# Ranking slots of stored tiles later in the free list of a hybrid decoder kernel

## The chip, the cores and the metric

The kernel runs on one core of a Trainium2 chip. The metric is the device time of one execution in microseconds (us); the time before is 1214.88 us, the median of three runs.

## The reference

One decoder layer is applied to x (1024 positions by 1024 channels, fp32). A normalised and modulated input goes through one wide projection. Its columns feed two gated linear recurrences in parallel (HGRN2 with 8 heads, GLA with 4 heads). Each branch is normalised, gated and projected, the branches are merged by sigmoid gates, projected once more, added to x and normalised.

```python
h = rms_norm(x, norm_w[l]) * (1.0 + scale[:, None, :]) + shift[:, None, :]
proj = h @ w_in[l]
hq, hf, hi, hz, gq, gk, gv, gz, ga, mg = jnp.split(proj, IN_OFFSETS, axis=-1)
y_h = hgrn2_branch(hq, hf, hi, hz, lb_all[l], hgrn_norm_w[l])
y_g = gla_branch(gq, gk, gv, gz, ga, gla_alpha_w[l], gla_alpha_b[l], gla_norm_w[l])
u_h = y_h @ w_branch[l, 0]
u_g = y_g @ w_branch[l, 1]
mg = jax.nn.sigmoid(mg.reshape(B, T, N_BRANCH, D_MODEL))
merged = mg[:, :, 0] * u_h + mg[:, :, 1] * u_g
x = x + gate[:, None, :] * (merged @ w_out[l])
return rms_norm(x, final_norm_w)
```

Inside a branch the recurrence S_t = diag(a_t) S_{t-1} + k_t v_t^T, o_t = S_t^T q_t is computed in chunks.

## The kernel before

**Arithmetic.** Every large product is made from three matmuls on operands that are split into a rounded high part and a remainder. `split` (L191) does it for one tile: a ScalarE cast (L196) makes the high part, a VectorE subtraction (L197) the low part. In the last stages the same is done by `build` (cast L1263, subtraction L1264) and `prep_duo` (cast L1285, subtraction L1286), for blocks that are multiplied in seven products instead of eight; for these, sums and differences of blocks are made earlier and kept in memory.

**Storage.** Nearly all working tiles of SBUF come from 46 slots of 128 partitions by 4 KB. `Slots.get` takes the slot at the head of a list of free slots, `Slots.free` puts slots back at its end, so the slot that was free longest is taken first. `Halves` hands out halves of such a slot. All this happens while the program is written, not while it runs. The tile framework then makes the first instruction that writes a new tile wait for the last instruction that used the slot before, also for the landing of a store that still reads it.

**Order.** After an opening that is written by hand, the framework orders the instruction lists of TensorE (PE), VectorE (DVE), ScalarE (ACT), GpSimd (POOL) and SyncE (SP, which issues the loads) by times that it plans for them. Which slot a tile has enters this plan, since it decides on whom the tile's first writer waits.

**Stages.** `Stream` (L857) runs one projection job after another, PE's matmuls being L541 (feature tiles) and L600 to L602 and L643 to L645 (value tiles). It weaves two other tracks between them: the attention of the heads (`attention`, L657; PE scores L683, L715, L770, L776, L781; DVE work on them L690 to L759), and a background track with `factors` (L1155: loads of stored activations, differences L1166, stores L1167) and `weight_sums` (L1183: loads L1189, sums L1195 to L1199, stores L1201). The last stages (from about 750 us) multiply the blocks (L1343), take snapshots of PSUM banks (`snap_of`, L1315 and L1317), and apply the gates (L1414).

**Stores.** Five places write a tile to memory and give its slot back at once, while the store is still to run: `put_act` (L914, results yh and yg of a branch), `factors`, `weight_sums`, `put_gate1` (L1412, a gate) and `drop_wy` (L1487, sums of the output weights). All are issued by POOL.

Of the kernel before, what the change touches and what calls it, by code (L numbers as in the profile page):

```python
# [2 lines left out]

# [31 lines left out]
class Slots:  # L35


    def __init__(self, pool, n):
        self.pool = pool
        self.free_list = deque(range(n))  # L40
        self.owner = {}
        self.serial = 0

    def get(self, shape, dtype=F32):
        i = self.free_list.popleft()
        self.serial += 1
        t = self.pool.tile([P] + list(shape), dtype, tag=f"s{i}", name=f"b{self.serial}")
        self.owner[id(t)] = (i, t)
        return t

    def free(self, *tiles):
        for t in tiles:
            self.free_list.append(self.owner.pop(id(t))[0])


class Halves:
# [5 lines left out]
    def get(self):  # L62
        if not self.open:
            t = self.slots.get([2, 512])
            left = [0, t]
            self.open.extend((t[:, i, :], left) for i in range(2))
        v, left = self.open.popleft()
        left[0] += 1
        self.owner[id(v)] = (v, left)
        return v  # L70

    def free(self, *views):
        for v in views:
            v, left = self.owner.pop(id(v))
            left[0] -= 1
            if left[0]:
                self.open.append((v, left))
            else:
                self.open = deque(z for z in self.open if z[1] is not left)
                self.slots.free(left[1])  # L80


@with_exitstack
def hybrid_trunk_kernel(
# [7 lines left out]
    x2, o2 = x[0], out[0]  # L92
# [8 lines left out]
    S = Slots(sp, N_SLOTS)  # L101
    Q = Halves(S)
# [811 lines left out]
    def put_act(acts, d, y):  # L914
        for half in range(2):
            nc.gpsimd.dma_start(acts[half][d // 2][:, d % 2 * 512:d % 2 * 512 + 512], y[:, half * 512:half * 512 + 512])
        S.free(y)

    def alpha_side():
        lower_bound()  # L920
# [49 lines left out]
    def gla_attention(h):  # L970
        qk = g_state
        v = qk.pop(("v", h))
        g = {}
        sq = {}

        def post(vh, half, po):
            if half == 0:
                g[vh] = qk.pop(("z", h, vh))
                sq[vh] = S.get([T])
            sl = slice(half * 512, half * 512 + 512)  # L980
            nc.scalar.activation(sq[vh][:, sl], po, AF.Square)
            nc.vector.scalar_tensor_tensor(g[vh][:, sl], po, vec[:, R_GN + vh:R_GN + vh + 1],
                                           g[vh][:, sl], ALU.mult, ALU.mult)

        yield from attention(qk.pop(("q", h)), qk.pop(("k", h)), alphas[h], lambda: v, 0, 256, post)
        S.free(*v)
        nc.gpsimd.tensor_add(sq[0], sq[0], sq[1])
        yield 1.5
        rst = sq[1]
        yield from inverse_root(rst, sq[0], 256)  # L990
        for half in range(4):
            sl = slice(half * 256, half * 256 + 256)
            for vh in range(2):
                nc.vector.tensor_mul(g[vh][:, sl], g[vh][:, sl], rst[:, sl])
            yield 1.5
        for vh in range(2):
            put_act(yg_d, 2 * h + vh, g[vh])
        S.free(*sq.values())
# [142 lines left out]
    def part_of(acts, kh, half, kk):  # L1141
        return acts[half][kh * 2 + kk]
# [12 lines left out]
    def factors(acts, f):  # L1155
        sub = nc.vector.tensor_sub
        for kk in range(2):
            while len(S.free_list) < 12:
                yield 1
            y = {}  # L1160
            for b in ("12", "11", "22", "21"):
                y[b] = S.get([T])
                nc.sync.dma_start(y[b], part_of(acts, int(b[0]) - 1, int(b[1]) - 1, kk))
            yield 6
            for p, dst, a, b in ((5, "11", "12", "11"), (7, "12", "12", "22"), (6, "22", "22", "11"), (4, "21", "21", "22")):
                sub(y[dst], y[a], y[b])  # L1166
                nc.gpsimd.dma_start(f[p][kk], y[dst])  # L1167
                if p == 7:
                    S.free(y["12"])
                elif p == 6:  # L1170
                    S.free(y["11"])
                yield 1.5
            S.free(y["22"], y["21"])

    def branch(n, d):
        return w_branch[0, n, :, d * P:(d + 2) * P]
# [6 lines left out]
    def weight_sums(b, i):  # L1183
        src = sources[b][i]
        while len(S.free_list) < 12:
            yield 1
        x1, x2 = S.get([4, 2, P]), S.get([4, 2, P])
        for kh, x in enumerate((x1, x2)):
            nc.sync.dma_start(x.rearrange("p k a f -> p k (a f)"),  # L1189
                              src[kh * 512:(kh + 1) * 512, :].rearrange("(k p) f -> p k f", p=P))  # L1190
        yield 6
        s1, s2 = S.get([2, 4, P]), S.get([2, 4, P])
        parts = {5: s1[:, 0], 6: s1[:, 1], 3: s2[:, 0], 7: s2[:, 1]}
        add = nc.vector.tensor_add
        add(parts[7], x1[:, :, 0], x1[:, :, 1])  # L1195
        add(parts[5], x1[:, :, 1], x2[:, :, 1])
        yield 1.5
        add(parts[6], parts[7], x2[:, :, 1])
        add(parts[3], parts[6], x2[:, :, 0])  # L1199
        for p, q in SUMS.items():  # L1200
            nc.gpsimd.dma_start(w_sums[b][i // 2][q][:, i % 2 * 512:i % 2 * 512 + 512],  # L1201
                                parts[p].rearrange("p k f -> p (k f)"))
        S.free(x1, x2, s1, s2)
        yield 3

    def prepare():
        yield from factors(h_d, f_x)
        for b in range(4):
            for i in range(4):
                yield from weight_sums(b, i)  # L1210
# [79 lines left out]
    class Banks:  # L1290
# [11 lines left out]
        def free(self, v):  # L1302
            self.free_list.append(v)
# [108 lines left out]
    def put_gate1(d, half, ap, summed):  # L1412
        g = ap if summed else Q.get()
        nc.scalar.activation(g, ap, AF.Sigmoid)  # L1414
        nc.gpsimd.dma_start(gate1_d[d][:, half * 512:half * 512 + 512], g)
        Q.free(g)

    def put_gate0(d, half, ap, summed):
        nc.scalar.activation(merged(d, half), ap, AF.Sigmoid)
# [13 lines left out]
    def put_m(d, half, ap, summed):  # L1433
# [16 lines left out]
    for g in BUILT[1:]:  # L1450
        n = GROUPS.index(g)
# [8 lines left out]
    wy, w4_raw, W4 = {}, {}, {}  # L1460
# [24 lines left out]
        keep_wy(p, kk, *dst)  # L1485

    def drop_wy():  # L1487
        S.free(*wy.values())
        wy.clear()

    def load_w4(p):
# [97 lines left out]
    for kk, (lead, first, then) in enumerate((((0, 3, 0), (0, 6), (0, 7)), ((1, 1, 2), (1, 5), (1, 6)))):  # L1589
        after(*lead, lambda kk=kk: load_wy(kk))  # L1590
        after(*((1, 1, 0) if kk == 0 else (1, 7, 3)), drop_wy)
        for n in range(4):
            after(*first, n, lambda kk=kk, n=n: gate_wy(kk, n))
            after(*then, n, lambda kk=kk, n=n: sum_wy(kk, n))
# [124 lines left out]
```

## Time and profile before

| what | value |
|---|---|
| three runs | 1214.5, 1214.88, 1215.29 us |
| profiled execution, own time | 1216.46 us |
| its span | 1214.8 us |
| granted TensorE clock, mean | 0.998 |
| PE busy | 1184.1 us, 97% of the span |
| DVE busy | 790.9 us, 65% |
| ACT busy | 546.9 us, 45% |
| POOL busy | 123.8 us, 10% |
| moved by DMA | 183.51 MB, 151 GB/s on average |

The profiled execution's own time exceeds its span by 1.66 us and the median of the three runs by 1.58 us. Times of instructions are those of this one execution. A row of the timeline gives start, duration, engine, source line and operation, then the tiles written and read without their numbers, and in brackets how long the engine sat idle before it and for whom. Adjacent instructions of one engine overlap by about 0.1 us.

### The profile page before, as it was taken

What the parts mean: (1) busy time and instruction counts of PE and PEld (TensorE: products, weight loads), DVE (VectorE), ACT (ScalarE), POOL (GpSimd) and SP (SyncE); (2) the same over time, 40 slices, a digit from 0 to 9 for tenths busy, and PEclk for the clock granted to TensorE, in tenths of its full rate; (3) what the DMA queues carried; (4) which work ended last, traced back from release to release, by engine and by line L of the source; (5) the groups of instructions that cost most, each with busy time, mean ns of one, the idle gap of its engine ahead of it and who ended that gap; (6) DMA issues with size and microseconds to landing.
All of it is one profiled execution on the core that took longest, in us unless ns stands there. A gap on an engine that the chain in (4) does not pass through costs nothing.

```text
span 1214.8 us, 20860 instructions
## 1 busy us (share of the span) xinstructions
PE 1184.1 (97%) x8579; PEld 982.6 (81%) x8579; DVE 790.9 (65%) x1245; ACT 546.9 (45%) x797; POOL 123.8 (10%) x215
## 2 busy tenths in 40 slices
PE   5999999999999999999999999999999999999997
PEld 3777889889798888888887888877778888878886
DVE  4637444774848456877884365794653775988994
ACT  5646732434434244344332324455743544444554
POOL 4100000202111121121110101011220000000000
PEclk9999999999999999999999999999999999999999
DMA  9814000844444267255341112054697746435523
GB/s 320 277 70 139 18 19 19 293 141 161 156 152 149 66 207 249 94 179 169 108 174 47 59 53 70 36 174 158 227 343 277 260 160 208 135 104 173 174 104 122
DMA packets 130961, 183.51 MB, mean 151 GB/s; under 512 B 7467, under 2 KB 97633, under 8 KB 130866
## 3 DMA queue, kind: packets, MB, share of 16 engines
q1 hardware_dynamic: 117250, 136.87, 35.7%
q0 software_dynamic: 13568, 45.31, 9.6%
q8 instruction: 67, 1.10, 0.4%
q14 instruction: 28, 0.23, 0.1%
q10 hardware_dynamic: 48, 0.01, 0.0%
HBM read 132.87 MB, written 49.28 MB: 150 GB/s over the span
## 4 chain that ended last, share of the span: by engine, by line
PE 61%; issue 23%; DVE 3%; ACT 3%; POOL 2%; DMA 1%; POOLq 0%; ACTq 0%; DVEq 0%
PE pd L541 19%; PE pd L1343 9%; PE sc_ps L1343 5%; PE pm L1343 5%; PE pd L1520 3%; PE pd L643 2%; PE pd L644 2%; PE pd L645 2%; PE sc_ps L1520 2%; PE pm L848 1%; PE pd L352 1%; PE pm L829 1%; PE pm L850 1%; PE pm L1520 1%; PE sc_ps L352 1%
## 5 line engine op out<-in xcount | busy, mean ns | idle before, releaser
L541 PE MATMUL pd<-b,b 128*128 128x512 f32 x1632 | 387.4, 394 | 0.0
L541 PEld LDWEIGHTS pd<-b,b 128*128 128x128 f32 x1632 | 302.4, 188 | 64.8 <-issue 1.4
L1343 PE MATMUL pd<-b,b 128*128 128x512 f32 x720 | 173.7, 392 | 4.3 <-ACT b L1414 2.1
L1343 PEld LDWEIGHTS pd<-b,b 128*128 128x128 f32 x720 | 133.7, 188 | 35.7 <-ACT b L1414 3.2
L197 DVE TENSOR_TENSOR b<-b,b 128x1024 fp32r<-128x1024 f32 (+2 forms) x89 | 98.9, 1122 | 83.1 <-ACT b L196 65.4
L196 ACT CAST b<-b 128x1024 fp32r<-128x1024 f32 (+2 forms) x89 | 82.9, 948 | 92.1 <-DVE b L1199 14.6
L1286 DVE TENSOR_TENSOR b<-b,b 128x1024 fp32r<-128x1024 f32 x56 | 68.3, 1224 | 66.9 <-ACT b L1285 52.3
L1285 ACT CAST b<-b 128x1024 fp32r<-128x1024 f32 x56 | 58.3, 1050 | 73.9 <-PE pd L1343 20.6
L1343 PE MATMUL sc_ps<-b,b 128*128 128x512 f32 x324 | 79.4, 391 | 1.0 <-ACT scT L793 1.0
L600 PE MATMUL pd<-b,b 128*128 128x256 f32 x256 | 74.2, 290 | 0.0
L1264 DVE TENSOR_TENSOR b<-b,b 128x1024 fp32r<-128x1024 f32 x48 | 59.2, 1251 | 20.8 <-ACT b L1263 15.1
L602 PE MATMUL pd<-b,b 128*128 128x256 f32 x256 | 72.5, 283 | 0.0
L601 PE MATMUL pd<-b,b 128*128 128x256 f32 x256 | 72.4, 283 | 0.0
L1343 PEld LDWEIGHTS sc_ps<-b,b 128*128 128x128 f32 x324 | 60.3, 188 | 14.6 <-ACT scT L793 1.4
L1343 PE MATMUL pm<-b,b 128*128 128x512 f32 x300 | 72.1, 389 | 0.0
L1263 ACT CAST b<-b 128x1024 fp32r<-128x1024 f32 x48 | 49.9, 1050 | 41.2 <-PE pd L1343 16.0
L1343 PEld LDWEIGHTS pm<-b,b 128*128 128x128 f32 x300 | 56.3, 188 | 11.7
L352 PE MATMUL pd<-b,b 128*128 128x512 f32 x192 | 53.3, 410 | 2.0 <-ACT b L196 0.9
L1201 POOL DMA_DIRECT2D ws<-b x64 | 34.6, 541 | 192.0 <-DVE b L1195 86.5
L735 ACT COPY xb<-b 128x512 f32<-128x512 f32 x48 | 29.4, 620 | 49.4 <-PE sc_ps L715 26.7
L643 PE MATMUL pd<-b,b 128*128 128x512 f32 x128 | 51.3, 401 | 0.0
L644 PE MATMUL pd<-b,b 128*128 128x512 f32 x128 | 50.0, 390 | 0.0
(285 smaller groups left out, 1964.3 us busy)
## 6 DMA issues: line engine op xcount, KB each, us to landing
b<-in_w_in_dram SPq DMA_DIRECT2D x66, 512.0 KB, 4.2
ws<-b POOLq DMA_DIRECT2D x64, 256.0 KB, 3.3
b<-ws SPq DMA_DIRECT2D x32, 512.0 KB, 4.9
b<-in_x_dram SPq DMA_DIRECT2D x16, 512.0 KB, 5.7
b<-in_ada_w_dram SPq DMA_DIRECT2D x32, 256.0 KB, 6.9
b<-in_w_branch_dram SPq DMA_DIRECT2D x16, 512.0 KB, 4.4
b<-h SPq DMA_DIRECT2D x14, 512.0 KB, 4.3
wo<-b POOLq DMA_DIRECT2D x14, 512.0 KB, 5.7
```

The lines of the kernel that those rows point to most:

```text
L196: nc.scalar.copy(hi, src)
L197: nc.vector.tensor_sub(lo, src, hi.bitcast(F32))
L352: nc.tensor.matmul(accs[f], wg(a, d, f), b[d][:, half * 512:half * 512 + 512], start=(d == 0 and n == 0), stop=(d == KT - 1 and n == 2))
L541: nc.tensor.matmul(ps[0:w, th * 512:(th + 1) * 512], a[:, k, 0:w], b[:, th * 512:(th + 1) * 512], start=(k == 0 and n == 0), stop=(k == KT ...
L600: nc.tensor.matmul(o, lh, hi[:, k % 4, :], start=(k == 0), stop=False)
L601: nc.tensor.matmul(o, lh, lo[:, k % 4, :], start=False, stop=False)
L602: nc.tensor.matmul(o, ll, hi[:, k % 4, :], start=False, stop=(k == KT - 1))
L643: nc.tensor.matmul(o, lh, hi[:, k % 2, :], start=(k == 0), stop=False)
L644: nc.tensor.matmul(o, lh, lo[:, k % 2, :], start=False, stop=False)
L1286: nc.vector.tensor_sub(lo, t, hi.bitcast(F32))
L1343: nc.tensor.matmul(o, a[:, sl], c, start=(p in (1, 5) and kt == 0 and n == 0), stop=(kt == 3 and n == 2), skip_group_check=True)
L1520: nc.tensor.matmul(o, a, b, start=(p in (1, 5) and kt == 0 and n == 0), stop=(kt == 3 and n == 2), skip_group_check=True)
```

## The change

The list of free slots becomes a heap. A slot's rank is the count of tiles taken so far when it is given back; slots of tiles that were given back behind a store to memory (`sent=True`) have 8 added to it, so they rank behind slots that are given back up to eight takings later. Among equal ranks, the one given back first goes first. The number of slots, the moments at which tiles are taken and given back, and thus every count of free slots, are as before.

```diff
     def get(self, shape, dtype=F32):
-        i = self.free_list.popleft()
+        i = heapq.heappop(self.free_list)[-1]
...
-    def free(self, *tiles):
+    def free(self, *tiles, sent=False):
         for t in tiles:
-            self.free_list.append(self.owner.pop(id(t))[0])
+            self.freed += 1
+            heapq.heappush(self.free_list, (self.serial + (8 if sent else 0), self.freed, self.owner.pop(id(t))[0]))
...
     def put_act(acts, d, y):
...
-        S.free(y)
+        S.free(y, sent=True)
...
                 if p == 7:
-                    S.free(y["12"])
+                    S.free(y["12"], sent=True)
                 elif p == 6:
-                    S.free(y["11"])
+                    S.free(y["11"], sent=True)
                 yield 1.5
-            S.free(y["22"], y["21"])
+            S.free(y["22"], y["21"], sent=True)
...
-        S.free(x1, x2, s1, s2)
+        S.free(x1, x2)
+        S.free(s1, s2, sent=True)
...
-        Q.free(g)
+        Q.free(g, sent=True)
...
     def drop_wy():
-        S.free(*wy.values())
+        S.free(*wy.values(), sent=True)
```

`Halves.free` passes the mark on: a slot counts as sent if one of its two halves was. Of 853 tiles taken, 78 are given back as sent, and 272 tiles get a slot with another history than before. The first of them is b_2258, a load that SP issues at 238.00 us in the profile before.

Since the framework orders the instructions by its plan and the plan knows the slots, the lists of SP, DVE, ACT and POOL come out in another order too. Lines of the changed kernel have numbers higher by 4 or 5. Three places, each before and after:

**VectorE, the second GLA head's first score stage (about 236 us).** The rows L690 to L718 work on the scores of a head; b_2296 is the low part of a value-tile split whose high part is b_2295, and b_2275 and b_2277 are loads of `factors`. Before:

```order
L1003 COPY b_2088<-pd_2001 128x1024
L710 TENSOR_TENSOR xb<-b_660,tot_726 128x128x4
L690 TENSOR_TENSOR blk<-sc_ps,eye_679 128x256
L699 TENSOR_TENSOR b_664<-b_664,b_1055 128x256x3
L695 COPY_PREDICATED blk<-mask_683,sc_ps 128x64
L696 COPY_PREDICATED blk<-mask_683,sc_ps 128x64x2
L711 TENSOR_TENSOR xb<-xb,tot_726 128x64x4
L697 COPY_PREDICATED blk<-mask_683,sc_ps 128x64x2
L717 TENSOR_TENSOR b_660<-xb,tot_726 128x64x12
L698 COPY_PREDICATED blk<-mask_683,sc_ps 128x64
L718 TENSOR_TENSOR tot_726<-tot_726 128x64
L197 TENSOR_TENSOR b_2296<-b_2090,b_2295 128x1024
```

After:

```order
L1007 COPY b_2088<-pd_2001 128x1024
L201 TENSOR_TENSOR b_2296<-b_2090,b_2295 128x1024
L1170 TENSOR_TENSOR b_2277<-b_2275,b_2277 128x1024
L714 TENSOR_TENSOR xb<-b_660,tot_726 128x128x4
L694 TENSOR_TENSOR blk<-sc_ps,eye_679 128x256
L703 TENSOR_TENSOR b_664<-b_664,b_1055 128x256x3
L699 COPY_PREDICATED blk<-mask_683,sc_ps 128x64
L700 COPY_PREDICATED blk<-mask_683,sc_ps 128x64x2
L715 TENSOR_TENSOR xb<-xb,tot_726 128x64x4
L701 COPY_PREDICATED blk<-mask_683,sc_ps 128x64x2
L721 TENSOR_TENSOR b_660<-xb,tot_726 128x64x12
L702 COPY_PREDICATED blk<-mask_683,sc_ps 128x64
```

The subtraction for b_2296 and the difference b_2277 have moved from behind the score stage to ahead of it. The slots of b_2295 and b_2296 are now those of b_1116 and b_1200, two results yg which `put_act` stores; before, two loads (b_2258 and b_2275) had these slots.

**SyncE, the loads ahead of a GLA head (about 328 to 365 us).** Rows with in_w_in_dram are loads of weights; those of L1189 are for `weight_sums`. Before:

```order
L621 DMA b_3420<-in_w_in_dram 128x2x512
L1189 DMA b_3320<-in_w_in_dram 128x4x256
L523 DMA b_3695<-in_w_in_dram 128x8x128
L621 DMA b_3424<-in_w_in_dram 128x2x512
L621 DMA b_3422<-in_w_in_dram 128x2x512
L621 DMA b_3426<-in_w_in_dram 128x2x512
L1189 DMA b_3678<-in_w_in_dram 128x4x256
L1189 DMA b_3474<-in_w_in_dram 128x4x256
L1189 DMA b_3475<-in_w_in_dram 128x4x256
L523 DMA b_3552<-in_w_in_dram 128x8x128
L1189 DMA b_3679<-in_w_in_dram 128x4x256
```

After:

```order
L1193 DMA b_3320<-in_w_in_dram 128x4x256
L625 DMA b_3424<-in_w_in_dram 128x2x512
L625 DMA b_3420<-in_w_in_dram 128x2x512
L625 DMA b_3422<-in_w_in_dram 128x2x512
L625 DMA b_3426<-in_w_in_dram 128x2x512
L1193 DMA b_3678<-in_w_in_dram 128x4x256
L1193 DMA b_3679<-in_w_in_dram 128x4x256
L527 DMA b_3695<-in_w_in_dram 128x8x128
L1193 DMA b_3475<-in_w_in_dram 128x4x256
L1193 DMA b_3474<-in_w_in_dram 128x4x256
L527 DMA b_3552<-in_w_in_dram 128x8x128
```

The loads b_3420 and b_3695 have moved into the cluster, and b_3474 has moved from behind b_3678 to behind b_3679, b_3695 and b_3475. On VectorE in this stretch four rows of `weight_sums` (b_3567, b_3568 from b_3474, b_3475) and the first row of the next one (L1196, b_3818, in the slot of b_3567) now stand directly ahead of L710, and two of the three subtractions L197 that stood there have moved behind the score stage.

**ScalarE, last HGRN2 head beside the block products (about 846 to 853 us).** b_7887 is a snapshot of the PSUM bank pd_7440, which frees it for PE; b_7906 is the high part of a sum of squares, which POOL finishes at L1107. Before:

```order
L1263 CAST b_7941<-b_7890 128x1024
L1095 ACTIVATE b_7845<-pm_7837 128x512
L1095 ACTIVATE b_7845<-pm_7848 128x512
L1315 COPY b_7821<-sc_ps 128x512
L1263 CAST b_7940<-b_7889 128x1024
L1315 COPY b_7887<-pd_7440 128x512
L196 CAST b_7906<-b_4458 128x1024
```

After:

```order
L1099 ACTIVATE b_7845<-pm_7837 128x512
L1099 ACTIVATE b_7845<-pm_7848 128x512
L1320 COPY b_7821<-sc_ps 128x512
L200 CAST b_7906<-b_4458 128x1024
L1320 COPY b_7887<-pd_7440 128x512
L1268 CAST b_7940<-b_7889 128x1024
L1290 CAST b_7972<-b_7870 128x1024
```

The cast b_7906 now stands ahead of the snapshot b_7887, and the cast b_7941 no longer stands ahead of the two squares L1095.

More of the change, by code (lines that the diff above doesn't have):

```diff
@@ L1 @@
+import heapq
 from collections import deque
@@ L39, in __init__ @@
         self.pool = pool
-        self.free_list = deque(range(n))
+        self.free_list = [(-1, i - n, i) for i in range(n)]
+        self.freed = 0
         self.owner = {}
@@ L64, in get @@
             t = self.slots.get([2, 512])
-            left = [0, t]
+            left = [0, t, False]
             self.open.extend((t[:, i, :], left) for i in range(2))
@@ L70, in get, with free @@
         return v
-    def free(self, *views):
+    def free(self, *views, sent=False):
         for v in views:
@@ L75, in free @@
             left[0] -= 1
+            left[2] |= sent
             if left[0]:
@@ L79, in free @@
                 self.open = deque(z for z in self.open if z[1] is not left)
-                self.slots.free(left[1])
+                self.slots.free(left[1], sent=left[2])
 @with_exitstack
```

## The prediction

> **What bounds the kernel now.** I read the page first (busy times, the clock, the chain, the DMA issues), then PE's waits, then the timelines of the places where the built order differs.
>
> ```profile
> PE 1184.1 (97%) x8579; PEld 982.6 (81%) x8579; DVE 790.9 (65%) x1245; ACT 546.9 (45%) x797; POOL 123.8 (10%) x215
> PEclk9999999999999999999999999999999999999999
> ws<-b POOLq DMA_DIRECT2D x64, 256.0 KB, 3.3
> b<-in_w_in_dram SPq DMA_DIRECT2D x66, 512.0 KB, 4.2
> ```
>
> PE is busy for 97% of the span, at nine tenths or more of its full clock in every one of the 40 slices. The change takes no matmul away, so it can win only PE's waits and lose wherever it makes new ones. The last two rows are medians from issue to landing: a 256 KB store takes 3.3 us, a 512 KB load 4.2. PE's waits between 80 and 1100 us, as total, times and longest:
>
> ```profile
> PE pd L1343 <- ACT b L1414: 2.1, 2, 1.8
> PE pd L1343 <- DVE b L953: 1.5, 1, 1.5
> PE sc_ps L1343 <- ACT scT L793: 1.0, 1, 1.0
> PE sc_ps L715 <- DVE tot L718: 0.7, 1, 0.7
> ```
>
> These are nearly all there is: about 5 us in the four rows, 0.4% of the time. Two of them end behind a store (places D and E below) and are what the change can take away. A new wait counts as soon as it is longer than the slack that the waiting row has ahead of PE, and at the places below this slack is 0.1 to 2.1 us. A time difference of 0.2% is 2.4 us; the three runs of before lie within 0.8 us.
>
> **What the change moves.** It adds and removes no instruction. The lists of tiles show that the slots do go to others, and the built order shows that SP, DVE, ACT and POOL run in another order, so that it does nothing, or leaves the order as it was, is excluded. What a slot loses in one place another gains: a taker that no longer waits for a store leaves that store's slot to a later one. So the sum goes place by place. Durations are those of the profiled execution, 1216.46 us.
>
> **Place A, second GLA head, 236 to 254 us.** First VectorE, then PE, then the four stores of the first head's results, the loads that waited for them, and the DMA traffic from 228 to 240 us.
>
> ```profile
> 236.38 1.22 DVE L1003 COPY b<-pd 128x1024 f32<-128x1024 f32 x1
> 237.51 0.68 DVE L710 TENSOR_TENSOR xb<-b,tot 128x512 f32<-128x512 f32 x1
> ...
> 241.34 0.43 DVE L698 COPY_PREDICATED blk<-mask,sc_ps 128x64 f32<-128x64 int32 x1
> ...
> 241.69 1.26 DVE L197 TENSOR_TENSOR b<-b,b 128x1024 fp32r<-128x1024 f32 x1
> ...
> 244.05 1.23 DVE L1166 TENSOR_TENSOR b<-b,b 128x1024 f32<-128x1024 f32 x1 [0.93 <-issue]
> ...
> 252.87 0.18 DVE L759 COPY_PREDICATED blk<-mask,sc_ps 128x32 f32<-128x32 int32 x1
> ```
> ```profile
> 243.91 0.89 PE L715 MATMUL sc_ps<-xb,b 128*32 128x48 f32 x64
> ```
> ```profile
> 253.20 0.66 PE L770 MATMUL sc_ps<-xb 128*16 128x16 f32 x62
> ```
> ```profile
> L916 POOL DMA_DIRECT2D yg<-b x4: 539/542/544, 230.4 to 232.2; - x4
> ...
> DMA to landing us min/median/max: 5.3/5.9/7.1
> ```
> ```profile
> 238.00 0.38 SPq L523 DMA_DIRECT2D b<-in_w_in_dram  x1
> 239.36 0.32 SPq L1163 DMA_DIRECT2D b<-h  x1
> ```
> ```profile
> DMA packets 1946, 4.76 MB, mean 397 GB/s; under 512 B 178, under 2 KB 939, under 8 KB 1945
> ```
>
> The last store is issued at 232.2 and with the 7.1 us of the slowest lands at 239.3. The two loads that had the slots of the stored tiles before went out at 238.00 and 239.36, the second right at that landing. They are late, but nobody on PE's path needed them soon. Now the split's cast and subtraction (b_2295, b_2296) take these slots, so VectorE's L197 for b_2296 cannot start before 239.3, and the order has put it, and an L1166, ahead of L710. Queued behind are the whole score stage L710 to L698 and through it PE's L715. The working: 239.3 plus 1.26 and 1.23 less 0.08 of overlap each is 241.6 for L710, 4.1 later than 237.51. L698 ends 241.77 - 237.51 = 4.26 after L710 starts, so at 245.9. L715 stood at 243.91, with a slack of 2.1 behind L698; it comes about 2.0 late. The lower end: were the stores to land in the page's 3.3 us, at 235.5, L197 would follow L1003 at 237.5 and L698 would end at 244.1, 0.3 late with the passing on. The upper end: two weight loads that waited now go out sooner, among the stores. 512 KB at 397 GB/s is 1.3 us each, so 2.0 plus 2.6 is 4.6. I take 2.0 plus half of one load, 2.7, since this stretch is already at the rate of the row and only part of the traffic stands in front.
>
> A rule of the Trainium skill speaks the other way: the page "DMA: Bandwidth & Descriptors", section "Anatomy of one DMA — SWDGE (gpsimd) path", gives a transfer issued by GpSimd about 2.0 us plus its bytes over 436e3. For 256 KB this is an estimate of 2.6 us, by which the stores land by 234.8 and place A costs its lower end of 0.3. The trace, with 5.3 to 7.1 us for these four stores, disagrees: it bears out no such time while loads share the traffic.
>
> PE's L770 at 253.20 has no slack (L759 ended at 253.05). One more load late among the L1166s there costs up to 1.3 and nothing at least; I take 0.5.
>
> **Place B, the third GLA head, 366 to 383 us.**
>
> ```profile
> 367.24 2.77 DVE L994 TENSOR_TENSOR b<-b,b 128x256 f32<-128x256 f32 x8 [5.13 <-ACT b L967]
> ...
> 372.27 0.68 DVE L1198 TENSOR_TENSOR b<-b,b 128x512 f32<-128x512 f32 x1
> ...
> 377.31 0.69 DVE L710 TENSOR_TENSOR xb<-b,tot 128x512 f32<-128x512 f32 x1
> ...
> 381.14 0.43 DVE L698 COPY_PREDICATED blk<-mask,sc_ps 128x64 f32<-128x64 int32 x1
> ```
> ```profile
> 382.38 0.89 PE L715 MATMUL sc_ps<-xb,b 128*32 128x48 f32 x64
> ```
> ```profile
> 373.25 0.54 POOL L1201 DMA_DIRECT2D ws<-b  x1 [0.66 <-DVE b L1198]
> ```
>
> L698 ends at 381.57, so the slack is 0.81. Now VectorE does after L994 (370.01) one L197 and three sums, which ends L1198 at about 373.0; its store goes out 0.3 later as in the row of POOL, at 373.3. The next weight sum, L1196 for b_3818, stands ahead of L710 and writes the slot that this store reads. With the store at 3.3 us it starts at 376.6 and L710 at 377.2, no later than before: the lower end, 0. With the 5.9 us of place A it starts at 379.2, L710 at 379.8, 2.5 late, less 0.81 is 1.7. With 7.1 it is 2.9, and with half a load for b_3474, which is now issued behind three others, 3.5: the upper end. Loads are bunched here too, so I take 1.7.
>
> **Place C, 846 to 854 us.** ScalarE, PE, POOL:
>
> ```profile
> 846.46 1.04 ACT L1263 CAST b<-b 128x1024 fp32r<-128x1024 f32 x1 [3.92 <-DMA b<-fx]
> 847.41 1.08 ACT L1095 ACTIVATE b<-pm 128x512 f32<-128x512 f32 x2
> ...
> 850.46 0.58 ACT L1315 COPY b<-pd 128x512 f32<-128x512 f32 x1
> 852.22 1.05 ACT L196 CAST b<-b 128x1024 fp32r<-128x1024 f32 x1 [1.18 <-POOL b L1107]
> ```
> ```profile
> 851.11 2.98 PE L1343 MATMUL pd<-b,b 128*128 128x512 f32 x12
> ```
> ```profile
> 849.64 2.55 POOL L1107 TENSOR_TENSOR b<-b,b 128x1024 f32<-128x1024 f32 x1
> ```
>
> PE's L1343 at 851.11 follows the snapshot L1315 (end 851.04) with 0.07 to spare. Now the cast L196, which waits for POOL's L1107 until 852.22, stands ahead of that snapshot: 852.22 plus 1.05 plus 0.58 less an overlap of 0.1 is 853.75, against 851.04 2.7 later. That is the upper end. But the cast of 846.46, which waited for a load, no longer stands ahead of the two L1095, and POOL's L1107 can start up to 1.4 earlier (the second L1095 begins when PE's head is done, about 847.7, and not at 848.0 behind the first; VectorE and POOL's store follow from the first). So I take 1.3; if the rows on PE that follow can go first, nothing is lost.
>
> **ScalarE at 817 us.** The changed order has a cast L1260 between the two snapshots of the second row:
>
> ```profile
> 809.29 1.04 ACT L1260 ACTIVATE b<-b 128x1024 fp32r<-128x1024 f32 x1
> ...
> 817.24 1.08 ACT L1317 ACTIVATE b<-pd 128x512 f32<-128x512 f32 x2
> ```
> ```profile
> 818.38 5.73 PE L1343 MATMUL pd<-b,b 128*128 128x512 f32 x24
> ```
>
> The snapshots end at 818.32, 0.06 ahead of PE. 1.04 more is the upper end, nothing the lower, if PE's first bank is the other one; half, 0.5.
>
> **What goes, D and E.**
>
> ```profile
> 892.22 0.60 ACT L1414 ACTIVATE b<-pd 128x512 f32<-128x512 f32 x1 [0.76 <-DMA gate<-b]
> ```
> ```profile
> 892.87 1.43 PE L1343 MATMUL pd<-b,b 128*128 128x512 f32 x5 [1.82 <-ACT b L1414]
> ```
> ```profile
> 305.98 0.69 DVE L1196 TENSOR_TENSOR b<-b,b 128x512 f32<-128x512 f32 x1 [3.56 <-DMA yg<-b]
> ```
> ```profile
> 313.46 0.89 PE L715 MATMUL sc_ps<-xb,b 128*32 128x48 f32 x64 [0.66 <-DVE tot L718]
> ```
>
> At E, L1196 waited 3.56 us for a stored result to land, and through the score stage this cost PE 0.66. Its tile now has a slot with no store behind it, so 0.66 goes; next late is nothing, as PE's own rows fill it. At D, the gate waited 0.76 for the store of another gate. That goes; the rest of PE's 1.82 is work queued ahead on ScalarE, so the gain is 0.76, between 0 and 1.82.
>
> **Elsewhere.** The rest of the 272 tiles I have not priced one by one. PE's slack elsewhere is as in A to C, so one more new wait of A's size, 2.7, is possible, rounded to 3; the freed wait for scT (1.0) bounds the gain. I take 0.7, the size of E's wait with the other sign, as new waits are the more likely where PE waits for so little now.
>
> **The sum.** 2.7 + 0.5 + 1.7 + 1.3 + 0.5 + 0.7 - 0.66 - 0.76 = 6.0 us. On the profiled execution's 1216.46 this is 1222.5; less the 1.58 by which that execution lies above the median, 1220.9 us.
>
> **The rivals.** *Crowded*: the loads that go out sooner push the stores back and A, L770, B, C and the cast at 817 take their upper ends: 4.6 + 1.3 + 3.5 + 2.7 + 1.0 + 0.7 - 1.42 = 12.4, so 1227.3 us. For it speaks that the stretch of place A already moves 397 GB/s; against it, that all must fall together. *Covered*: the stores land as fast as the page's 3.3 us, since their rivals among the loads have moved. Then A is 0.3, L770 and B are 0, the order of ScalarE (1.3 and 0.5) and elsewhere stay: 0.3 + 1.3 + 0.5 + 0.7 - 1.42 = 1.4, so 1216.3 us, not to be told from no change. Against it speak the 5.3 to 7.1 us. The 2.6 us per store of the Trainium skill's page "DMA: Bandwidth & Descriptors", weighed above, would lead here as well. *Faster*: only the waits behind stores matter, and the change removes them at D in full and at E: 1.82 + 0.66 = 2.5 gained, with nothing lost, 1216.46 - 2.5 - 1.58 = 1212.4 us. This decides if A's L197 can start by 237.5, so if its last store lands 1.8 us sooner than in the trace, and if ScalarE's orders cost nothing. For it speaks that fewer first writers stand behind a store; against it, that the first writers that now do stand behind one are VectorE rows ahead of a score stage.
>
> **How the numbers follow.** Forecast (about 2.5 to 9 more): 0.60. Crowded: 0.14. Covered: 0.15. Faster: 0.11. The likeliest gives 1220.9. The range takes in the forecast and most of crowded, up to 1227.5, and reaches below the covered case's 1216.3 to 1215.5, since A, B or C alone may be at its lower end; what it leaves out is the faster case and the ends of the others. Slower by over 2.4 us: forecast and crowded, 0.74. Within it: covered, 0.15. Faster: 0.11.
>
> **What would show it.** Right: in the changed kernel's profile L201 (b_2296) sits idle at about 238 us until a store of yg, and PE's wait list has L719, late by 2 to 3 us at about 246, and again at about 385; L1348 waits for a snapshot L1320 at about 852; the waits of E and D are gone. Wrong: no idle time ahead of L719 at A (then the stores landed early), or PE's waits in sum below 5 us. New waits at places not named here, of more than 3 us together, would show that the part elsewhere was missed.

## The result and the profile after

The changed kernel takes 1233.09 us (median of 4 runs, 1232.46 to 1235.17) against 1214.87 us before: a ratio of 1.0147, 95% interval 1.0132 to 1.0162. It is 18.2 us slower, where 6.0 had been forecast. The profiled execution took 1232.72 us, with a span of 1230.6, so 15.8 us more of span than before.

The page's line of busy times and PE's waits between 80 and 1110 us (total, times, longest), of the changed kernel. Line numbers are higher by 4 or 5 than before.

```profile
PE 1189.2 (97%) x8579; PEld 986.0 (80%) x8579; DVE 793.4 (64%) x1245; ACT 548.2 (45%) x797; POOL 122.9 (10%) x215
```
```profile
PE sc_ps L719 <- DVE tot L722: 7.0, 2, 4.2
PE pd L1348 <- DVE b L957: 4.0, 1, 4.0
PE sc_ps L687 <- DVE xb L683: 2.7, 2, 1.8
PE pd L1348 <- ACT b L1320: 1.5, 1, 1.5
PE pd L1348 <- ACT b L1419: 0.9, 2, 0.6
```

Two things are to be read here. PE's waits, of which the longest are shown, add up to 18.7 us instead of 7.3, which is 11.4 more. And PE is busy for 5.1 us more with the same 8579 matmuls: they ran more slowly. The views by stretches of 3 us show where; the columns are the stretch, its length, busy time (and instructions) of each engine, then PE's granted clock, DMA share and GB/s.

```profile
246.00:249.00 3.00, 1.08 (x56) 1.11 (x60) 3.00 (x8) 0.00 (x0) 0.00 (x0) 0.77 0.68 216
249.00:252.00 3.00, 3.00 (x31) 2.43 (x21) 2.93 (x8) 0.62 (x1) 1.20 (x3) 0.66 0.49 188
389.00:392.00 3.00, 1.71 (x66) 1.53 (x67) 3.00 (x7) 0.62 (x1) 0.00 (x0) 0.83 0.00 0
392.00:395.00 3.00, 3.00 (x9) 2.33 (x9) 3.00 (x6) 0.00 (x0) 0.17 (x1) 0.60 0.02 5
825.00:828.00 3.00, 1.03 (x4) 0.67 (x4) 3.00 (x4) 2.18 (x4) 0.00 (x0) 0.98 0.37 149
828.00:831.00 3.00, 3.00 (x8) 2.20 (x8) 3.00 (x8) 0.19 (x1) 0.00 (x0) 0.50 0.54 175
831.00:834.00 3.00, 3.00 (x14) 2.47 (x13) 2.40 (x8) 2.34 (x3) 0.00 (x0) 0.95 0.02 5
```

Behind each of the three longest waits the clock drops. The missing share times 3 us, summed over a place's rows, is 1.71 us at each of the three ((0.23 + 0.34) x 3, (0.17 + 0.40) x 3, (0.02 + 0.50 + 0.05) x 3): the loss of about 3.4 us at half clock. That is 5.1 us, and with the waits 16.5, against the 15.8 of the span. (The rest of the 18.2 between the medians: the execution profiled before lies 1.6 us above its median, the one after 0.4 below, and its time exceeds its span by 0.5 us more.)

Place A, VectorE, ScalarE, PE, and the time to landing of the loads of h that were issued from 231 us on, after and then before:

```profile
239.09 1.23 DVE L201 TENSOR_TENSOR b<-b,b 128x1024 fp32r<-128x1024 f32 x1 [5.09 <-ACT b L200]
242.39 1.23 DVE L1170 TENSOR_TENSOR b<-b,b 128x1024 f32<-128x1024 f32 x1 [2.07 <-DMA b<-h]
243.53 0.68 DVE L714 TENSOR_TENSOR xb<-b,tot 128x512 f32<-128x512 f32 x1
```
```profile
238.01 1.05 ACT L200 CAST b<-b 128x1024 fp32r<-128x1024 f32 x1 [2.18 <-DMA yg<-b]
```
```profile
247.92 1.51 PE L719 MATMUL sc_ps<-xb,b 128*32 128x48 f32 x64 [4.19 <-DVE tot L722]
```
```profile
L1167 SPq DMA_DIRECT2D b<-h x4: 319/338/412, 231.6 to 245.4; - x4
...
DMA to landing us min/median/max: 8.5/10.0/10.8
```
```profile
L1163 SPq DMA_DIRECT2D b<-h x3: 320/338/339, 231.8 to 239.4; - x3
...
DMA to landing us min/median/max: 4.6/5.5/6.4
```

L201 started at 239.09, 0.2 from the forecast 239.3, and waited for the stores as foretold, through its cast L200 on ScalarE, which waited 2.18 us for a store of yg. But the row behind it, the difference L1170, then waited 2.07 us more for a load of h. These loads took 8.5 to 10.8 us. Of those before, the one at 231.83, beside the same stores, took 6.4, and the one at 239.36 took 4.6; the profile has no landing of the third. Without this wait L714 would have started 2.07 us earlier.

Place B: VectorE, PE, how long SP stood at a semaphore ahead of the loads of `weight_sums` (shortest, median, longest, in ns), and for what:

```profile
379.32 0.69 DVE L1199 TENSOR_TENSOR b<-b 128x512 f32<-128x512 f32 x1 [4.18 <-DMA b<-in_w_in_dram]
...
385.30 0.69 DVE L1200 TENSOR_TENSOR b<-b,b 128x512 f32<-128x512 f32 x1 [3.36 <-DMA ws<-b]
385.91 0.68 DVE L714 TENSOR_TENSOR xb<-b,tot 128x512 f32<-128x512 f32 x1
```
```profile
390.29 0.96 PE L719 MATMUL sc_ps<-xb,b 128*32 128x48 f32 x64 [2.79 <-DVE tot L722]
```
```profile
L1193 SPq EVENT_SEMAPHORE  x5: 17/17/7858, 359.5 to 370.4; - x5
```
```profile
SPq L1193 <- DMA ws<-b: 7.9, 1, 7.9
```

Both waits stand ahead of L714: 4.18 us for a load and 3.36 for the store. SP stood still for 7.86 us ahead of a load whose slot was behind a store (ws), and the loads queued behind it came late.

Near 553 us a sum waits for a load ahead of L683; at 818 us a first writer stands behind a store of yh, and PE's L1348 waits for L957 behind it:

```profile
553.89 0.69 DVE L1199 TENSOR_TENSOR b<-b 128x512 f32<-128x512 f32 x1 [1.74 <-DMA b<-in_w_branch_dram]
```
```profile
819.43 1.23 DVE L1269 TENSOR_TENSOR b<-b,b 128x1024 fp32r<-128x1024 f32 x1 [1.40 <-DMA yh<-b]
```
```profile
826.97 5.25 PE L1348 MATMUL pd<-b,b 128*128 128x512 f32 x14 [3.98 <-DVE b L957]
```

Places C and D came as forecast in kind: at C PE waits 1.46 us for the snapshot L1320 (0.16 before), at D 0.63 us instead of 1.82:

```profile
869.19 3.01 PE L1348 MATMUL pd<-b,b 128*128 128x512 f32 x12 [1.46 <-ACT b L1320]
```
```profile
909.32 3.02 PE L1348 MATMUL pd<-b,b 128*128 128x512 f32 x12 [0.63 <-ACT b L1419]
```

### The profile page after: what moved, and what is told of

The parts are those of the page before. It is cut to its first block, busy times and chain, and to the rows that moved or that the text cites. A ratio compares the mean times of both kernels' runs of the same rounds, so it can differ in the third digit from the quotient of the medians.

```text
span 1230.6 us, 20846 instructions
## 1 busy us (share of the span) xinstructions
PE 1189.2 (97%) x8579; PEld 986.0 (80%) x8579; DVE 793.4 (64%) x1245; ACT 548.2 (45%) x797; POOL 122.9 (10%) x215
## 4 chain that ended last, share of the span: by engine, by line
PE 61%; issue 22%; DMA 3%; POOL 3%; DVE 3%; ACT 2%; POOLq 0%; SPq 0%; ACTq 0%; DVEq 0%
PE pd L545 17%; PE pd L1348 10%; PE sc_ps L1348 5%; PE pm L1348 5%; PE pd L1525 3%; PE pd L606 2%; PE pd L605 2%; PE pd L604 2%; POOL ws L1205 2%; PE pm L852 2%; PE sc_ps L1525 2%; PE pm L854 1%; DMA b<-in_w_in_dram 1%; PE pd L356 1%; PE pd L647 1%
## 5 line engine op out<-in xcount | busy, mean ns | idle before, releaser
L1348 PE MATMUL pd<-b,b 128*128 128x512 f32 x720 | 175.3, 394 | 6.9 <-DVE b L957 4.0
L1348 PEld LDWEIGHTS pd<-b,b 128*128 128x128 f32 x720 | 134.9, 189 | 38.8 <-DVE b L957 4.4
L201 DVE TENSOR_TENSOR b<-b,b 128x1024 fp32r<-128x1024 f32 (+2 forms) x89 | 100.5, 1140 | 77.6 <-ACT b L200 66.3
L200 ACT CAST b<-b 128x1024 fp32r<-128x1024 f32 (+2 forms) x89 | 82.9, 948 | 110.0 <-DMA yh<-b 18.0
L1348 PE MATMUL sc_ps<-b,b 128*128 128x512 f32 x324 | 79.3, 391 | 0.5 <-ACT scT L797 0.5
L1269 DVE TENSOR_TENSOR b<-b,b 128x1024 fp32r<-128x1024 f32 x48 | 57.8, 1220 | 23.5 <-ACT b L1268 12.7
L1348 PE MATMUL pm<-b,b 128*128 128x512 f32 x300 | 72.1, 389 | 0.0
L1348 PEld LDWEIGHTS sc_ps<-b,b 128*128 128x128 f32 x324 | 60.3, 188 | 14.1 <-ACT scT L797 0.9
L1348 PEld LDWEIGHTS pm<-b,b 128*128 128x128 f32 x300 | 56.3, 188 | 11.7
```

What stands on the lines that cost most here:

```text
L200: nc.scalar.copy(hi, src)
L201: nc.vector.tensor_sub(lo, src, hi.bitcast(F32))
L1348: nc.tensor.matmul(o, a[:, sl], c, start=(p in (1, 5) and kt == 0 and n == 0), stop=(kt == 3 and n == 2), skip_group_check=True)
```

## The experiments

Times of the experiments stand against runs of the kernel before on the same chip, whose median there was 1215.95 to 1217.47 us, so the ratios are what counts. All are edits of the changed kernel unless said otherwise.

**The change in four parts, by the count of takings at which a slot is given back.** The built orders of the four kernels differ from the kernel before almost only at their own places, so each shows one part alone.

```diff
-8 if sent else 0
+8 if sent and self.serial < 155 else 0            # w1_first
+8 if sent and 155 <= self.serial < 245 else 0     # w2_b
+8 if sent and 245 <= self.serial < 360 else 0     # w3_c
+8 if sent and self.serial >= 360 else 0           # w4_d
```

> Only slots given back before the 155th taking are ranked later; its order differs from the kernel before at place A alone. Local theory (each new wait of PE comes from the slots given back just ahead of it, and a long wait costs clock after it): PE waits 4.2 at the second GLA head's L719, then runs slow for about 1.3 us more, nothing else new, so +5.5 us (1220.4). Rival, the changed ranking spreads and costs everywhere: +10 or more. Rival, clock loss has nothing to do with waits: +4.2.

> Only slots given back between the 155th and the 245th taking are ranked later. Local theory: 2.8 us wait at place B with about 1.6 of slow clock behind it, 0.4 near 342, and the gain of 0.66 at E: +4.1 us (1219.0). Rival, the wait at B needs the delay from place A: no wait at B, +0 or a gain of 0.7.

> Only slots given back between the 245th and the 360th taking are ranked later. Local theory: waits of 0.9 and 1.8 us at the score stages near 507 and 553, no slow clock behind these as they are under 2 us: +2.6 us (1217.5). Rival, they are consequences of the earlier delays: within 0.5 of the kernel before.

> Only slots given back from the 360th taking on are ranked later. Local theory: the wait for L957 near 811 grows by 2.5 and slows the clock for about 1.5 more, place C adds 1.3, D and the wait for scT give back 1.2 and 0.45: +3.7 us (1218.6). Rival, as before without slow clock: +2.2.

| part | time, us | ratio | 95% interval | PE's new waits there, us |
|---|---|---|---|---|
| w1_first | 1222.53 | 1.0050 | 1.0031 to 1.0069 | A 4.55, L957 2.35 (1.49 before) |
| w2_b | 1223.44 | 1.0054 | 1.0036 to 1.0072 | near 336 0.74, B 2.91, near 457 0.76 |
| w3_c | 1220.67 | 1.0031 | 1.0016 to 1.0045 | near 253 0.96, near 498 1.59, near 544 1.29 |
| w4_d | 1218.43 | 1.0019 | 1.0008 to 1.0030 | L957 3.05, C 1.46 |

By the ratios the parts cost 6.1, 6.6, 3.8 and 2.3 us, where 5.5, 4.1, 2.6 and 3.7 were expected: right in place, not in size. They add up to 1.54%, the whole change has 1.47%, which the intervals allow. Each of the change's long waits comes back in the part that gives back the slots just ahead of it, without the others; two smaller ones, near 253 in w3_c and near 457 in w2_b, are not in the whole change. The rivals of a spreading cost, and of a wait at B or later that needs the earlier delays, fall. In w1_first the clock is 0.50 and 0.57 in the two stretches behind the wait at A; in w3_c it stays at 1.00 behind 1.59 us, but falls at 649 us, where PE had not waited (see the clock below).

**Place A: the store or the load.** In a_far the two slots behind the stores of yg rank so late that no split takes them; the L1170 ahead of L714 stays, and SP issues the loads of h in one group as in the whole change, but 2.6 us later, from 234.2 us on. In a_behind the slots are those of the first part, but the four differences keep their program order, which is behind the score stage.

```diff
+24 if sent and self.serial < 140 else 0           # a_far
...
# a_behind: the first part, and in factors, for f_x and kk == 1
-                sub(y[dst], y[a], y[b])
+                tc.keep_in_program_order(sub(y[dst], y[a], y[b]))
```

> Place A alone, but the two slots behind the stores of yg rank 24 takings later, so that no split takes them: the cast and the subtraction L201 at A wait for no store; the order on VectorE (L201 and one L1170 ahead of L714) and the three loads that go out early stay. Theory load (the loads that went out early are slow, and the L1170 that waits for them is the binding wait): PE still waits about 4 us at L719, +5 us in all (1221). Theory store (the wait for the stores of yg is what counts): PE waits at most 0.5, within 1 us of the kernel before.

> Place A alone, with the slots of the change there, but the four differences L1170 of the second half are kept in program order, which puts them behind the score stage; L201 still waits for the stores of yg ahead of L714. Theory load: L714 starts at about 240.2, PE waits about 0.5 at L719 and no slow clock follows, +0.5 to 1 us (1216.5). Theory store: about the wait of the first part, 4 us, and +5 us.

a_far: 1222.78 us, ratio 1.0058 (1.0038 to 1.0079). a_behind: 1218.93 us, ratio 1.0017 (1.0004 to 1.0030). VectorE at A, first of a_far, then of a_behind, and PE's waits from 230 to 260 us of the two:

```profile
235.57 1.23 DVE L201 TENSOR_TENSOR b<-b,b 128x1024 fp32r<-128x1024 f32 x1 [5.17 <-ACT b L200]
...
242.07 1.23 DVE L1170 TENSOR_TENSOR b<-b,b 128x1024 f32<-128x1024 f32 x1 [4.14 <-DMA b<-h]
```
```profile
237.97 1.23 DVE L201 TENSOR_TENSOR b<-b,b 128x1024 fp32r<-128x1024 f32 x1 [4.85 <-ACT b L200]
239.11 0.69 DVE L714 TENSOR_TENSOR xb<-b,tot 128x512 f32<-128x512 f32 x1
```
```profile
PE sc_ps L719 <- DVE tot L722: 5.0, 1, 5.0
```
```profile
PE sc_ps L719 <- DVE tot L722: 0.7, 1, 0.7
```

In a_far L201 starts 3.5 us earlier and PE waits as long as ever, now for the load alone (the loads, issued later, took 7.2 to 7.9 us and landed at about the same time). In a_behind L201 waits until the stores have landed and PE waits 0.7; its time is 2 us above the kernel before and not 0.5 to 1, and its profile has a wait of 2.35 us for L957 with half clock behind it. So at place A the row that decides is the difference that waits for a load and stands ahead of the score stage. The wait for the stores, on which the forecast rested, is hidden beneath it.

**The clock.** The kernel before, with memsets repeated ahead of a matmul of the opening:

```diff
-        nc.vector.memset(pg, 0.0)
+        for _ in range(n + 1 if half == 0 else 1):
+            nc.vector.memset(pg, 0.0)
```

> The kernel before with twelve more memsets of a PSUM tile ahead of one matmul at about 95 us, which make PE wait about 2.5 us there and nothing else. Theory clock (a wait of over about 2.3 us is followed by some 3.4 us at half clock): a stretch at 0.5 to 0.7 behind the wait, 2.5 + 1.7 = 4.2 us more. Rival (the slow clock belongs to the places, not to the wait): 2.5 us more and full clock.

> The same with 22 memsets: a wait of about 6.6 us. Theory clock, with a slow stretch of fixed length: 6.6 + 1.7 = 8.3 us more. Rival, a slow stretch in proportion to the wait: 6.6 + 4 = 10.6. Rival without clock: 6.6.

> The kernel before with three more memsets; twelve had made PE wait 8.2 us at 67 us and 22 made it 14.9, so 0.67 us each above 0.2: a wait of about 2.2 us. Theory clock with a limit just above 2 us that depends on the moment: either no slow clock or one stretch of 3.4 us at half clock; a mean of 0.75 would need a limit that is no such thing.

The first two missed their lengths: the matmul stands at 67 us, not 95, where the memsets have little cover, and PE waited 8.2 and 14.9 us (n of 12 and 22), and 2.2 with n of 3. So the total times (1224.43, 1232.03 and, in one run, 1219.76 us) don't test the sums as written. The clock does. Stretches behind the wait, first of n of 3, then of 12, then of 22:

```profile
69.00:72.00 3.00, 2.10 (x12) 0.49 (x16) 2.44 (x5) 0.15 (x1) 0.00 (x0) 0.63 0.00 0
72.00:75.00 3.00, 3.00 (x16) 1.34 (x9) 1.23 (x1) 2.84 (x5) 0.00 (x0) 0.80 0.00 0
```
```profile
75.00:78.00 3.00, 2.64 (x16) 0.49 (x16) 2.07 (x4) 0.70 (x2) 0.00 (x0) 0.50 0.00 0
78.00:81.00 3.00, 3.00 (x22) 1.98 (x14) 1.22 (x1) 3.00 (x5) 0.00 (x0) 0.99 0.00 0
```
```profile
84.00:87.00 3.00, 3.00 (x15) 1.02 (x8) 1.01 (x2) 2.65 (x5) 0.00 (x0) 0.50 0.00 0
87.00:90.00 3.00, 3.00 (x18) 2.35 (x17) 2.02 (x4) 3.00 (x7) 0.54 (x1) 0.98 0.28 116
```

A wait of 2.2 us, made at a place that had 0.2, brings the slow clock: it belongs to the wait, not to the place. PE resumes at 69.9, 75.4 and 82.4 us. In the last two the clock has fallen while PE still waits, at 71.23 and 70.08 us, and it rises again at 78.06 and 87.15, so that PE works at half clock for another 2.7 and 4.7 us, and for 3.3 with n of 3. From fall to rise these are 3.41, 6.83 and 17.07 us: one, two and five times 3.41. All stretches of half clock between 30 and 1200 us, in all 18 profiles, are such multiples: one at each of the changed kernel's three places, two at place A in w1_first, a_far, before_behind and lag_24.

Taking the moments at which the clock changes in a profile as marks of a grid of 3.41 us (in best_ends the rise in the opening, at 21.34 us), one sees which waits bring it. In the 18 profiles there are 17 windows of these grids at full clock in which PE was busy for 1.50 us or less, and each is followed by half clock; of those in which it was busy for 1.64 to 3.3 us, none is. So it counts how much of a wait falls into one window. Of a wait of 2.35 us in a_behind 1.9 us do, and half clock follows; one of 2.34 us in best_ends (below) is shared by two windows, and none follows:

```profile
810.52:813.94 3.42, 1.50 (x7) 1.25 (x8) 3.42 (x6) 1.24 (x3) 0.00 (x0) 1.00 0.12 50
813.94:817.35 3.41, 3.41 (x10) 2.63 (x9) 3.41 (x8) 0.54 (x1) 0.00 (x0) 0.50 0.48 154
```
```profile
806.41:809.82 3.41, 2.05 (x34) 1.33 (x23) 3.41 (x4) 2.33 (x4) 0.00 (x0) 1.00 0.86 334
809.82:813.24 3.42, 2.43 (x11) 2.00 (x12) 3.42 (x7) 0.86 (x2) 0.00 (x0) 1.00 0.14 22
813.24:816.65 3.41, 3.41 (x28) 2.59 (x30) 3.34 (x8) 1.45 (x3) 0.00 (x0) 1.00 0.38 143
```

Three more stretches of 3.41 us follow no wait: w3_c at 648.8, lag_24 at 663.1 and stall22 at 660.6 us. In the window ahead of each, PE was busy throughout, mostly with eight matmuls on the tile `ones`. The other profiles have the same eight at full clock afterwards; what sets the three apart stays open. In w3_c this is 1.7 us of loss that no wait caused.

**The order in the whole change and in the kernel before.** Differences and sums of the background track keep their program order, in the changed kernel (all_behind) and in the kernel before (before_behind):

```diff
-                sub(y[dst], y[a], y[b])
+                tc.keep_in_program_order(sub(y[dst], y[a], y[b]))
...
-        add(parts[7], x1[:, :, 0], x1[:, :, 1])
+        tc.keep_in_program_order(add(parts[7], x1[:, :, 0], x1[:, :, 1]))
...
```

> The whole change, but the differences of factors and the sums of weight_sums keep their program order on VectorE, behind the score stages of places A and B; slots, the order on SP and the stores are nearly those of the change. Theory order (PE's new waits up to 600 us come from background rows that wait for a load or a store and stand ahead of a score stage): the waits of 4.2, 2.8, 0.9 and 1.8 us and two slow stretches go, about 12 of the 18 us; the part from 800 us on stays: +4 to +6 us. Rival (waits of the casts and splits for stores do it, wherever the sums stand): +14 or more.

> The kernel before with the same rows kept in program order, to see what that order costs or brings by itself. Theory order: no new long wait, within 2 us of the kernel before (it can win the 0.7 us of place E). Rival: the rows come too late now and their stores with them, +3 us or more.

all_behind: 1219.04 us, ratio 1.0024 (1.0014 to 1.0033). Of the 1.47%, 1.23 percentage points are gone. Between 110 and 800 us PE's waits are now

```profile
PE sc_ps L774 <- DVE blk L763: 0.5, 1, 0.5
PE pm L833 <- ACT b L812: 0.2, 1, 0.2
PE sc_ps L719 <- DVE blk L702: 0.2, 1, 0.2
```

with the slots of the change in place. before_behind: 1222.41 us, ratio 1.0054 (1.0033 to 1.0075), a miss. Its VectorE shows at A

```profile
241.60 1.23 DVE L197 TENSOR_TENSOR b<-b,b 128x1024 fp32r<-128x1024 f32 x1 [5.29 <-DMA fx<-b]
```

a subtraction that stands inside the score stage, in a slot whose store (fx) comes later now that the differences come later: it is among two stores issued at 232 and 233 us, where the kernel before issues this group from 223 to 228. PE waits 3.57 us there. So the program order is no cure by itself: order and slots have to fit. With the slots of the change, the fitting order takes the cost away up to 800 us; with those of before, it makes one.

**Eight or 24.** The whole change with 24 takings.

> The whole change with 24 in place of 8. Theory order: stores are avoided better, but the slots and with them the built order change again, with new rows that wait ahead of score stages: slower than before by 5 to 20 us. Theory store: what matters is the distance of the stored slots, so with 24 nearly all waits behind stores go: within 3 us of the kernel before or faster.

1233.92 us, ratio 1.0146 (1.0126 to 1.0167): no better than 8, with other waits. At A PE waits 4.8 us, and at 478 us a ScalarE cast that waits for a load stands ahead of the copies that PE needs:

```profile
478.00 1.04 ACT L200 CAST b<-b 128x1024 fp32r<-128x1024 f32 x1 [8.01 <-DMA b<-in_w_in_dram]
```

PE loses 5.0 us there. The forecast by order held, the one by distance did not: distance from the stores alone brings nothing here.

**From 800 us on.** w4_one_slot is the fourth part without the slot of yh that L1269 takes, late_only ranks later only from the 500th taking on; best_early and best_ends are all_behind with the ranking before the 360th taking only, and there and from the 500th on.

```diff
+8 if sent and self.serial >= 360 and self.serial != 429 else 0   # w4_one_slot
+8 if sent and self.serial >= 500 else 0                          # late_only
+8 if sent and self.serial < 360 else 0                           # best_early
+8 if sent and not 360 <= self.serial < 500 else 0                # best_ends
```

> The part from the 360th taking on, without the one slot that is given back at the 429th (behind a store of yh), which a low half of a product's factors (L1269) then takes. Theory store at this place: L1269 no longer waits 1.4 us for the store near 808, PE's wait for L957 is 1.5 again with no slow clock behind it; about 3 us less than the whole part. Theory order: the wait stays at 3.

> The change alone without rows in program order, only for slots given back from the 500th taking on (gates and sums of output weights). Theory: it does here what it is for, ScalarE's L1419 waits for no gate store at 892 and PE wins 1.2 us; 1.0 to 1.5 us faster. Rival: another row takes the place of that wait, no gain.

> The same with later ranking only before the 360th taking: the wait of D stays, so 1.2 us more than the run above and about 1 us faster than the kernel before. Rival: same time as the run above, D's wait is hidden elsewhere.

> The change with background rows in program order, and with later ranking only for slots given back before the 360th and from the 500th taking on. If the parts add up: all_behind less the waits at 811 (3.3, of which 1.5 are in the kernel before, and 1.7 of slow clock) and 854 (1.3): no wait that the kernel before lacks, the waits of E (0.7), near 521 (0.4) and D (1.2) gone: about 2 us faster than before, 1214 against 1216. Rival (the order costs elsewhere): +1 or more.

| kernel | time, us | ratio | 95% interval |
|---|---|---|---|
| w4_one_slot | 1218.05 | 1.0007 | 0.9997 to 1.0016 |
| late_only | 1215.81 | 0.9995 | 0.9985 to 1.0004 |
| best_early | 1215.19 | 0.9990 | 0.9981 to 0.9999 |
| best_ends | 1214.72 | 0.9984 | 0.9975 to 0.9993 |

VectorE ahead of L957 in w4_d, then in w4_one_slot:

```profile
806.05 1.23 DVE L1269 TENSOR_TENSOR b<-b,b 128x1024 fp32r<-128x1024 f32 x1 [1.45 <-DMA yh<-b]
```
```profile
804.12 1.23 DVE L1269 TENSOR_TENSOR b<-b,b 128x1024 fp32r<-128x1024 f32 x1
```

The wait of 1.45 us for the store goes with the one slot, but PE's wait for L957 falls only from 3.05 to 2.41 us, not to the expected 1.5. It is 2.35 too in w1_first and a_behind, which change nothing there, and 1.47 to 1.49 in w2_b, w3_c and late_only. The rows ahead show the difference. POOL's addition L1111 runs beside one of two VectorE rows, which then takes longer; first w4_d, then w4_one_slot:

```profile
798.02 0.62 DVE L689 TENSOR_TENSOR b<-b,b 128x256 f32<-128x256 f32 x1
```
```profile
797.39 3.09 DVE L689 TENSOR_TENSOR b<-b,b 128x256 f32<-128x256 f32 x1
```

In w4_d it is L683 that takes 2.20 us in place of 0.63, in w4_one_slot L689, and the two rows together take 0.9 us more in the second. The changed kernel, w1_first, a_behind and best_ends are like w4_one_slot here; the kernel before, w2_b, w3_c, late_only, best_early and all_behind are like w4_d. So the store costs all of the 1.6 us that w4_d has above 1.5, and the row beside POOL 0.9 us where it is L689. Which of the two it is does not follow from the order of VectorE's rows, which is the same; with one profile of each kernel, what decides it stays open.

At D the change does what it is for: in late_only PE's wait is 0.60 us, and the time is 0.8 us lower, within its uncertainty. best_ends is faster than the kernel before by 0.16%, about 1.9 us, and best_early by 0.10%; between the two the intervals don't tell, and both gains are smaller than the 4.3 us by which single runs of the kernel before differ.

## Why the prediction was wrong

The direction and most places were right, the size was not: 18.2 us, outside the range to 1227.5. Two steps failed. The sum put the clock behind a long wait at nothing, and that was 5.1 us; and it priced the new rows ahead of a score stage by their stores and their work, not by the loads for which they wait. The signs that were named for being right came, L719's waits among them, so they could not tell 6 us from 18. The terms one by one, in us:

| term | forecast | in the profile after |
|---|---|---|
| A, L719 | 2.7 | 4.19 |
| L770 behind it | 0.5 | 0 |
| B | 1.7 | 2.79 |
| C | 1.3 | 1.30 |
| ScalarE at 817, then L957 | 0.5 | 2.5, for another reason |
| elsewhere (0.91, 1.79 and smaller ones of both signs) | 0.7 | 2.5 |
| E and D | -1.42 | -1.85 |
| slow clock | no term | 5.1 |

- **The missing term.** That a long wait is followed by a slow clock had no term at all. Three waits of 2.8 to 4.2 us cost 1.7 each on top. The trace before showed no slow clock between 30 and 1200 us: its longest wait from 110 us on was 1.82, and its least busy window of 3.41 us still had 2.02 us of PE's work. The Trainium skill has the rule, in the page "TensorE: Matmul & The Clock Gate", section "HAM oscillation — how this bites in real kernels": no idle gaps of PE over some 3.4 us. By that limit B with 2.79 would have gone free; the runs decide otherwise and show the slow clock behind 2.2 and 2.79 us, and none behind 1.8. Behind 2.3 to 2.4 us it came in w1_first, a_behind and w4_one_slot and not in best_ends and before_behind, by how much of the wait fell into one window of 3.41 us. The length agrees at the three places: the section "What's actually happening" gives a window of 3413 ns and half the rate, an estimated loss of 1.71 us, and they have 1.71.
- **A.** The step that the stores hold L201 until 239.3 was right to 0.2 us, and it was not the binding one. The early loads were a side term, half of 1.3 us. In fact they took about 10 us beside the stores and each other, and L1170, which waits for one, stands behind L201 and ahead of L714; a_far and a_behind show that this row decides. The order that is quoted ahead of the prediction shows it there; I priced its 1.23 us of work and hardly its wait.
- **B.** The wait for the store was priced at 1.7 us of PE's time; VectorE waited 3.36 for it. The load was priced only within the upper end; VectorE waited 4.18 for it, behind the 7.86 us that SP stood at a load bound to a store. Both waits were covered in part by subtractions that had moved away.
- **Around 817 us.** The cast between the snapshots was not what came late. A store of yh, in the slot of a low half, was (1.40 us of VectorE's time), and the row beside POOL's L1111 took 0.9 us longer than in the trace before.
- **Elsewhere.** The two waits for L683 (0.91 and 1.79) are of the kind of A and B, sums that wait ahead of a score stage. There was no row for them in the sum. With the 0.38 near 342 us they make 3.1 us, just over the 3 that the prediction named as the sign of a missed part.
- **C, D, E.** Right in place and nearly in size; that C came to 1.3 exactly is luck, since 1.3 was taken between 0 and 2.7. The faster rival had its gains (1.85) and lost on what it excluded.
- **Crowded.** The rival at 1227.3 named the mechanism of place A, loads and stores that slow each other, with too short a wait and no clock.

## What to carry to other kernels

A change of which buffer a tile gets is a change of the instruction order where a planner orders by buffers. Ask which rows now stand ahead of the ones that the busiest engine waits for, and price their waits, the loads first, not their work. A wait that left TensorE 1.50 us or less of work in a window of 3.41 us cost 1.7 us and more on top, so one long wait was worse here than several short ones. Avoiding the slots of running stores pays where no order changes for the worse (D); with the rows that wait kept behind the score stages and the middle part left out, it gave 0.16%.

## What the runs showed of the hardware

- TensorE's clock fell to half for 3.41 us or for two or five times that. It did so behind each window of 3.41 us in which TensorE was busy for 1.50 us or less, and behind none with 1.64 to 3.3 us. In waits this means: behind 2.2 and behind 2.8 us or more each time, behind 2.3 to 2.4 in three of five, behind 1.8 or less never. At each of the changed kernel's three places 1.7 us were lost.
- Beside one addition of POOL (128x1024, 2.4 to 2.75 us) a VectorE row of 128x256 took 2.2 or 3.1 us instead of 0.63.
- In the kernel before, one of two loads of 512 KB that were issued beside four stores took 6.4 us; in the changed kernel three of them, behind another load, took 8.5 to 10.8 us beside the same stores. The traffic as a whole hardly differed, at 397 GB/s before and 404 after in the stretch from 228 to 240 us:

```profile
DMA packets 2771, 4.85 MB, mean 404 GB/s; under 512 B 191, under 2 KB 1885, under 8 KB 2770
```
